# Two-layer diffusion backbone on one core: each engine's instruction order set by an event-by-event timing simulation instead of the scheduler's default model

## The chip, the cores and the metric

The kernel runs on one core of one Trainium2 chip. The metric is the device time of one execution in microseconds (us); the number that counts is the median of several runs. Beside the timed runs there is one execution taken by the hardware profiler, whose page and trace are read below. PE is TensorE (matrix multiplies), PEld its weight loads, DVE is VectorE, ACT is ScalarE, POOL is GpSimd, and SP is the engine that issues nearly all transfers.

## The reference

Two post-norm layers over 1024 latent tokens and 256 context tokens of width 1024, all in float32. Layer 0 (stage A below) is windowed grouped-query attention with a sink and rotary positions, layer 1 (stage B) is neighbourhood attention on a 16 x 64 grid with a relative bias. Both have a gate path. Cut to what matters:

```
for i in range(DEPTH):                       # DEPTH = 2
    shift, scale, gate = split(silu(c) @ w_ada[i] + b_ada[i], 3)
    u  = h * (1 + scale) + shift             # the same for the context tokens uc
    q, k, v, g = split(u @ w_in)
    s  = q @ k.T / 8  (+ mask or bias, + columns of the context, + sink)
    o  = softmax(s) @ v
    y  = (o * silu(g)) @ w_out
    h  = layer_norm(ALPHA * h + gate * y)
```

## The kernel before

**Precision.** Every float32 operand of a large product is split into a high part `hi` and a remainder `lo`, and the product is made of three matmuls: hi*hi, hi*lo and lo*hi. So each split costs an ACT cast (the high part) and a DVE or POOL subtraction (the low part).

**Stages.** From 0 to about 120 us the modulation vectors, the modulated tokens `uA` and the keys and values of layer 0 are made (lines 440 to 610). Stage A, about 120 to 620 us, is the attention of layer 0: 8 head pairs p, 10 blocks b of 128 queries, 2 heads each, which gives 160 softmaxes, numbered k in the names (`S_A84` is the score tile of softmax 84). From about 590 to 750 us come the output projection of layer 0, its layer norm and the tokens `uB` of layer 1. Stage B, about 830 to 1375 us, is the attention of layer 1 with 128 softmaxes; the rest is the last output projection and layer norm.

**One softmax.** `qkA`/`qkB` (L685, L686, L1016, L1017) makes the scores `S` on PE in four matmuls. `sm_first` lets DVE add mask or bias and find the row maximum (L315), and ACT take the exponential and its sum (L322). `sm_second` lets DVE invert the sum (L326) and POOL scale the row (L327). `sm_transpose` lets PE transpose the row into the tile `T`, up to five times 128 x 128 (L334), then ACT casts it into the high part `pth`/`pt` (L338) and DVE subtracts for the low part `ptl`/`pt` (L340). At last `pv` multiplies the high and the low part by the values (L714 in A, L1044, L1047 and L1050 in B) for two softmaxes at once, a pair k and k+1. Score tiles and transposed tiles take turns in the same two PSUM buffers (tag `big`, `bufs=2`): a new `S` or `T` needs the buffer of an older one, which is free when DVE has read the scores (L315) or has read the transposed tile (L340).

**Fill.** In between, the projections of the next heads are made (`proj_pieces`, L207 to L209, tiles `pj`; `vproj_pieces`, L240 to L242, tiles `pv` with a weight number), three matmuls per piece. These are called fill below: they need no softmax. In stage A, DVE also makes 112 dot products for the modulation of layer 1 (L600, L601) and the rotation of the new queries.

**What sets the order.** `build` states the instructions in a program order in which `merge` and `att_steps` weave attention and fill together by costs written into the code. That is not yet the order on the engines. When the tile context closes, its scheduler plays the program forward in simulated time: when an engine is free, it takes the instruction of the highest priority among those that can go, and gives its output tile a buffer. Priority is the place in program order; `tc.high_priority(n)`, called `lift` here, raises it for some steps (`LIFT_A` 80, `LIFT_B` 40, 20 and 60 in `sm_transpose`). So the durations and waits of the scheduler's timing model decide which of two instructions stands first on an engine, and each engine runs its list in that fixed order. The only line that the change touches is in `kernel`, where the context is made:

## Time and profile before

| what | value |
|---|---|
| median of 3 runs | 1474.33 us (1472.61 to 1474.68) |
| the profiled execution's own time | 1476.44 us |
| its span, first to last instruction | 1474.7 us |
| busy: PE / DVE / ACT / POOL | 95% / 71% / 49% / 42% |
| mean granted TensorE clock | 0.983 |
| instructions | 24806, of them 8660 matmuls |

The span is 1.7 us shorter than the profiled execution's time, which is itself 2.1 us above the median. A matmul's recorded duration is longer than the step from its start to the next one's start, since matmuls are pipelined; the start times tell the pace.

### The profile page before, as it was taken

The page shows a single profiled execution, that of the slowest core. Times are in us where ns is not written, and L with a number is a line of the kernel's source. Part 1 is how long each engine was busy: PE and PEld are TensorE (multiplying, and loading weights), DVE is VectorE, ACT ScalarE, POOL GpSimd, SP SyncE. Part 2 cuts the span into 40 slices and gives each one's busy share as a digit, 9 for nine tenths or more (in the row PEclk, how much of TensorE's full clock was granted, in tenths as well). Part 3 has the DMA queues.
Part 4 walks back from the last instruction along what each step waited for, and adds up shares of the span by engine and source line. Part 5 has one row for each costly group of instructions (what it writes and reads, how often), then busy time and mean ns, then how long its engine had stood idle before and what let it go on. Part 6 is the DMA issues. An engine that isn't in the chain of part 4 may idle for free.

```text
span 1474.7 us, 24806 instructions
## 1 busy us (share of the span) xinstructions
PE 1401.7 (95%) x8660; PEld 1231.5 (84%) x8660; DVE 1048.1 (71%) x2339; ACT 715.9 (49%) x1481; POOL 620.1 (42%) x739
## 2 busy tenths in 40 slices
PE   7898999999999999999999999999999999998995
PEld 5797888888888788878888889888998899877784
DVE  6957999988998988666632565655565555677788
ACT  4525566666666668633222444554454444457300
POOL 3433655555655546423311232332233323345564
PEclk6999999999999999999999999999999999999998
DMA  8455222311412213333267355555555465564443
GB/s 308 160 191 149 65 90 80 122 62 54 134 45 75 90 49 119 115 128 131 91 191 209 95 162 153 151 171 140 163 159 162 131 177 150 143 191 123 140 118 91
DMA packets 117084, 194.51 MB, mean 132 GB/s; under 512 B 9312, under 2 KB 57824, under 8 KB 116960
## 3 DMA queue, kind: packets, MB, share of 16 engines
q1 hardware_dynamic: 116960, 192.92, 43.7%
q8 instruction: 69, 1.13, 0.3%
q14 instruction: 55, 0.45, 0.1%
HBM read 140.98 MB, written 51.90 MB: 131 GB/s over the span
## 4 chain that ended last, share of the span: by engine, by line
PE 62%; DVE 19%; issue 6%; ACT 5%; DMA 4%; POOL 3%; SPq 0%; DVEq 0%; ACTq 0%; POOLq 0%
PE pj L207 8%; PE pj L209 8%; PE pj L208 8%; PE T_B L334 4%; PE pvB L1047 4%; DVE s_A L315 3%; PE T_A L334 3%; DVE ptl_A L340 3%; PE pv L240 3%; PE pv L241 3%; PE pv L242 3%; PE S_B L1016 3%; PE yA L419 2%; PE yA L417 2%; PE yA L418 2%
## 5 line engine op out<-in xcount | busy, mean ns | idle before, releaser
L327 POOL TENSOR_SCALAR s_B<-s_B,rs_B 128x640 f32<-128x640 f32 (+1 forms) x128 | 101.6, 794 | 304.0 <-DVE rs_B L326 281.2
L207 PE MATMUL pj<-uBh,wh 128*128 128x512 f32 (+1 forms) x448 | 176.2, 393 | 0.0
L322 ACT ACTIVATE s_A<-s_A,m_A 128x641 f32<-128x641 f32 (+2 forms) x160 | 119.6, 747 | 116.7 <-DVE m_A L315 94.8
L208 PE MATMUL pj<-uBl,wh 128*128 128x512 f32 (+1 forms) x448 | 169.5, 378 | 0.0
L209 PE MATMUL pj<-uBh,wl 128*128 128x512 f32 (+1 forms) x448 | 169.4, 378 | 0.0
L327 POOL TENSOR_SCALAR s_A<-s_A,rs_A 128x640 f32<-128x640 f32 (+2 forms) x160 | 137.5, 860 | 73.3 <-DVE rs_A L326 69.6
L340 DVE TENSOR_TENSOR pt_B<-T_B,pt_B 128x640 fp32r<-128x640 f32 (+1 forms) x128 | 101.0, 789 | 84.1 <-ACT pt_B L338 83.7
L322 ACT ACTIVATE s_B<-s_B,m_B 128x640 f32<-128x640 f32 (+1 forms) x128 | 102.9, 804 | 116.2 <-DVE m_B L315 114.8
L207 PE MATMUL pj<-uAh,wh 128*128 128x512 f32 (+1 forms) x384 | 141.6, 369 | 0.0
L315 DVE CUSTOM_DVE_ANT_0 s_A<-S_A,msk,nsk 128x640 f32<-128x640 f32 (+2 forms) x160 | 123.6, 773 | 22.4 <-PE S_A L686 13.7
L209 PE MATMUL pj<-uAh,wl 128*128 128x512 f32 (+1 forms) x384 | 138.3, 360 | 0.0
L208 PE MATMUL pj<-uAl,wh 128*128 128x512 f32 (+1 forms) x384 | 137.7, 359 | 0.0
L165 POOL TENSOR_TENSOR wl<-wr,wh 128x512 fp32r<-128x512 f32 x64 | 88.6, 1386 | 100.4 <-ACT wh L163 94.2
L340 DVE TENSOR_TENSOR ptl_A<-T_A,pth_A 128x640 fp32r<-128x640 f32 (+2 forms) x160 | 113.8, 711 | 6.3 <-ACT pth_A L338 3.8
L338 ACT CAST pt_B<-T_B 128x640 fp32r<-128x640 f32 (+1 forms) x128 | 84.4, 659 | 67.3 <-PE T_B L334 66.7
L334 PE MATMUL T_A<-ident,s_A 128*128 128x128 f32 x672 | 101.3, 275 | 14.0 <-DVE m_A L315 7.4
L334 PEld LDWEIGHTS T_A<-ident,s_A 128*128 128x128 f32 x672 | 78.0, 141 | 40.3 <-issue 15.2
L315 DVE CUSTOM_DVE_ANT_0 s_B<-S_B,bias 128x640 f32<-128x640 f32 (+1 forms) x128 | 100.5, 785 | 10.4 <-PE S_B L1017 9.6
L338 ACT CAST pth_A<-T_A 128x640 fp32r<-128x640 f32 (+2 forms) x160 | 96.7, 604 | 19.4 <-PE T_A L334 16.4
L209 PEld LDWEIGHTS pj<-uBh,wl 128*128 128x128 f32 x448 | 84.2, 188 | 16.7
L334 PE MATMUL T_B<-ident,s_B 128*128 128x128 f32 x608 | 88.1, 274 | 9.9 <-DVE pt_B L340 6.2
L240 PE MATMUL pv<-wh,uBh 128*128 128x256 f32 x320 | 92.1, 288 | 0.9 <-ACT wh L163 0.9
(189 smaller groups left out, 3916.5 us busy)
## 6 DMA issues: line engine op xcount, KB each, us to landing
kB<-kdB SPq DMA_DIRECT2D x64, 320.0 KB, 5.5
gw<-in_wadaT SPq DMA_DIRECT2D x64, 256.0 KB, 2.8
vdB<-st SPq DMA_DIRECT2D x20, 512.0 KB, 3.3
vB<-vdB SPq DMA_DIRECT2D x16, 640.0 KB, 4.6
kdB<-st SPq DMA_DIRECT2D x16, 512.0 KB, 2.9
qdB<-st SPq DMA_DIRECT2D x16, 512.0 KB, 3.3
qB<-qdB SPq DMA_DIRECT2D x32, 256.0 KB, 4.7
ogr<-ogd SPq DMA_DIRECT2D x28, 256.0 KB, 3.0
```

The source lines that it names most:

```text
L165: e.tensor_tensor(lo, r, f32(hi), ALU.subtract)
L207: mm(pt[:, :n], hi[:, sl], rh, start=kt == 0, stop=False)
L208: mm(pt[:, :n], hi[:, sl], rl, start=False, stop=False)
L209: mm(pt[:, :n], lo[:, sl], rh, start=False, stop=kt == KT - 1)
L240: mm(pt, lh, hi[:, sl], start=kt == 0, stop=False)
L315: nc.vector.tensor_tensor_reduce(outp, sc, in1, scale, init if init is not None else 3e38, ALU.add, ALU.min, accum_out=s.m)
L322: nc.scalar.activation(s.t[:, :n], s.t[:, :n], AF.Exp, bias=s.m, scale=-1.0, accum_out=s.sum)
L327: nc.gpsimd.tensor_scalar(s.t[:, : s.w], s.t[:, : s.w], s.rs, 1.0, ALU.mult, ALU.mult)
L334: nc.tensor.transpose(tp[:, k * P : (k + 1) * P], s.t[:, src * P : (src + 1) * P], ident)
L338: nc.scalar.copy(pt.hi[:, :n, hl, :], tv)
L340: nc.vector.tensor_tensor(pt.lo[:, :n, hl, :], tv, f32(pt.hi[:, :n, hl, :]), ALU.subtract)
L1047: mm(ov[:, :, 1], v[:, t, :], x[:, k], start=not side and k + n == 0, stop=k == 3 and n == 1)
```

## The change

The scheduler's timing model is exchanged when the context is made. Nothing else in the program differs: the same instructions on the same engines, the same buffers and the same lifts.

```
-    with tile.TileContext(nc) as tc:
+    with tile.TileContext(nc, schedule_with_timeline_sim=True) as tc:
```

The changed order was read next to the old one. These are three places of it.

First PE in stage A, at the end of a pair (`T_A84`, `T_A85`). `pth_A82` and `pth_A84` are the high parts of the pairs 82/83 and 84/85, `ptl_A82` is the low part of the older pair, `pj` is fill. Before:

```order
L334 MATMUL T_A85_4604<-ident_63,s_A85_4504 128x128 x5
L207 MATMUL pj26_2_4598<-uAh2_109,wh26_3869 128x256
L208 MATMUL pj26_2_4598<-uAl2_112,wh26_3869 128x256
L209 MATMUL pj26_2_4598<-uAh2_109,wl26_3870 128x256
L685 MATMUL S_A88_4615<-kA2_0_3726,qA8_4040 128x384
L686 MATMUL S_A88_4615<-kA2_0_3726,qA8_4040 128x256
L685 MATMUL S_A88_4615<-kA2_1_4294,qA8_4040 128x384
L686 MATMUL S_A88_4615<-kA2_1_4294,qA8_4040 128x256
L207 MATMUL pj26_2_4598<-uAh2_109,wh26_3869 128x256
L208 MATMUL pj26_2_4598<-uAl2_112,wh26_3869 128x256
L209 MATMUL pj26_2_4598<-uAh2_109,wl26_3870 128x256
L714 MATMUL pvA4_0_4551<-pth_A82_4486,vA2_3770 128x256 x5
```

Here the pair that PE multiplies after `T_A85` is the older one, 82/83; the pair 84/85 follows only after `T_A87`. Now, the same place:

```order
L334 MATMUL T_A84_4568<-ident_63,s_A84_4467 128x128 x5
L685 MATMUL S_A87_4576<-kA2_0_3726,qA9_4041 128x384
L686 MATMUL S_A87_4576<-kA2_0_3726,qA9_4041 128x256
L685 MATMUL S_A87_4576<-kA2_1_4294,qA9_4041 128x384
L686 MATMUL S_A87_4576<-kA2_1_4294,qA9_4041 128x256
L714 MATMUL pvA4_0_4551<-ptl_A82_4487,vA2_3770 128x256 x5
L334 MATMUL T_A85_4604<-ident_63,s_A85_4504 128x128 x5
L685 MATMUL S_A88_4615<-kA2_0_3726,qA8_4040 128x384
L686 MATMUL S_A88_4615<-kA2_0_3726,qA8_4040 128x256
L685 MATMUL S_A88_4615<-kA2_1_4294,qA8_4040 128x384
L686 MATMUL S_A88_4615<-kA2_1_4294,qA8_4040 128x256
L714 MATMUL pvA4_2_4734<-pth_A84_4566,vA2_3770 128x256 x5
```

The fill has left the attention steps and stands in long runs before and after them, and the product of a pair follows its second transpose with only one score tile in between.

Second DVE in stage A, between the score tiles 85 and 86 (`s_A` is the row of a softmax, `m_A` its maximum, `gw`, `gj` and `dhalf` belong to the dot products of the next layer's modulation). Before:

```order
L315 ISA s_A85_4504,m_A85_4505<-S_A85_4499,msk_145,nsk_146 128x640
L315 ISA m_A85_4505 128x1
L340 TENSOR_TENSOR ptl_A82_4487<-T_A82_4488,pth_A82_4486 128x5x128
L724 TENSOR_TENSOR otmp_4516<-pvA3_8_4406,otmp_4516 64x256
L326 RECIPROCAL rs_A85_4507<-sum_A85_4506 128x1
L601 ISA gw_4559,dhalf_615<-gw_4559,gh_3895 128x512
L601 ISA dhalf_615 128x1
L315 ISA s_A86_4541,m_A86_4542<-S_A86_4536,msk_145,nsk_146 128x640
```

One dot product stands between the two score tiles, and the softmax steps follow each other closely. Now:

```order
L315 ISA m_A85_4505 128x1
L276 SCALAR_TENSOR_TENSOR gA4_4443<-th_4690,pj26_2_4598 128x256
L600 ISA gj_4745,dhalf_615<-gw_4743,gh_3900 128x512
L600 ISA dhalf_615 128x1
L326 RECIPROCAL rs_A85_4507<-sum_A85_4506 128x1
L601 ISA gw_4743,dhalf_615<-gw_4743,gh_3895 128x512
L601 ISA dhalf_615 128x1
L600 ISA gj_4818,dhalf_615<-gw_4816,gh_3900 128x512
L600 ISA dhalf_615 128x1
L601 ISA gw_4816,dhalf_615<-gw_4816,gh_3895 128x512
L601 ISA dhalf_615 128x1
L315 ISA s_A86_4541,m_A86_4542<-S_A86_4536,msk_145,nsk_146 128x640
```

Four dot products stand there now, while PE is in a run of fill.

Third SP at the start, the first transfers after the weights `wr0` and `wr1` (`wada` and `hraw` feed the modulation and the tokens; `cos`, `sin`, `nsk` and `msk` are tables that the attention needs). Before:

```order
L517 DMA wada_254<-in_wadaS 128x1024
L522 DMA hraw_256<-in_hT 128x1280
L149 DMA wr2_258<-in_wAk 128x512
L149 DMA wr3_260<-in_wAk 128x512
L517 DMA wada_304<-in_wadaS 128x1024
L517 DMA wada_306<-in_wadaS 128x1024
L522 DMA hraw_308<-in_hT 128x1280
```

The four tables come some twenty transfers later, behind the last `hraw`. Now:

```order
L517 DMA wada_254<-in_wadaS 128x1024
L522 DMA hraw_256<-in_hT 128x1280
L522 DMA hraw_308<-in_hT 128x1280
L574 DMA cos_143<-in_cos 128x1024
L575 DMA sin_144<-in_sin 128x1024
L576 DMA nsk_146<-in_sink 128x16
L578 DMA msk_145<-in_maskA 128x1152
L517 DMA wada_304<-in_wadaS 128x1024
L149 DMA wr2_258<-in_wAk 128x512
L149 DMA wr3_260<-in_wAk 128x512
L517 DMA wada_306<-in_wadaS 128x1024
```

The tables have moved ahead of the third pair of modulation weights and of the weights `wr2` and `wr3`.

Counted over the whole lists: between the second transpose of a pair and the first product of that pair there stood ten or more fill matmuls for 71 of the 80 pairs of stage A, and no pair was without fill there; now 71 pairs have none (15 of them context blocks with tiles of 256 columns). Between one transpose and the next there was never less than one fill piece in A; now 83 of the 159 steps have none. In stage B the pairs without fill before their product go from 7 to 28 of 64, and the softmaxes that are transposed after the last projection matmul go from 19 to 23.

## The prediction

> **What bounds the kernel now.** The page comes first: its span, the busy times and the granted clock in 40 slices.

> ```profile
> span 1474.7 us, 24806 instructions
> PE 1401.7 (95%) x8660; PEld 1231.5 (84%) x8660; DVE 1048.1 (71%) x2339; ACT 715.9 (49%) x1481; POOL 620.1 (42%) x739
> PEclk6999999999999999999999999999999999999998
> ```

> PE is busy for 95% and has 73.0 us of idle time in all (1474.7 - 1401.7). No matmul is added or removed, so a new order can win no more than these 73 us, and it loses what it adds to them. Where they lie, the windows tell (length, busy time of PE, PEld, DVE, ACT and POOL with counts, granted clock, DMA share, GB/s).

> ```profile
> 0.00:50.00 50.00, 34.79 (x155) 27.69 (x156) 37.51 (x51) 20.82 (x38) 22.74 (x12) 0.71 0.75 273
> 120.00:616.00 496.00, 473.90 (x3044) 413.42 (x3045) 437.03 (x1092) 315.99 (x678) 281.08 (x408) 1.00 0.28 86
> 1000.00:1100.00 100.00, 100.00 (x706) 93.25 (x705) 57.68 (x140) 48.89 (x103) 32.46 (x38) 1.00 0.53 150
> 1300.00:1400.00 100.00, 90.34 (x540) 76.72 (x539) 75.05 (x154) 56.70 (x117) 55.08 (x52) 1.00 0.50 146
> 1400.00:1475.00 75.00, 57.60 (x275) 47.97 (x273) 63.70 (x79) 4.44 (x8) 41.13 (x19) 0.91 0.40 105
> ```

> The start loses 15.2 us. Stage A loses 22.1 of 496 us, and DVE is nearly as full there (437.0 of 496, 88%). The middle of stage B loses nothing. Its end, where fill has run out, loses 9.7 us in 100, and the last projection 17.4. Stage A is thus where both engines are close to full, and where the order has changed most. The view of waits names what PE's weight loads wait for there (total, times, longest).

> ```profile
> PEld T_A L334 <- issue: 15.2, 31, 2.8
> PEld S_A L685 <- DVE ptl_A L340: 11.3, 22, 1.5
> PEld T_A L334 <- POOL s_A L327: 10.4, 16, 2.5
> ```

> The score tile `S_A` waits for DVE to empty a PSUM buffer, the transpose for its row. These are small sums over 160 softmaxes, because fill stands between dependent steps. The timeline shows it (start, duration, engine, line; in brackets the idle time before and its releaser).

> ```profile
> 343.31 0.82 DVE L340 TENSOR_TENSOR ptl_A<-T_A,pth_A 128x640 fp32r<-128x640 f32 x1
> 344.18 0.45 PE L685 MATMUL S_A<-kA,qA 128*128 128x384 f32 x1 [0.52 <-DVE ptl_A L340]
> ...
> 346.85 0.71 PE L334 MATMUL T_A<-ident,s_A 128*128 128x128 f32 x5
> 347.31 0.42 PE L685 MATMUL S_A<-kA,qA 128*128 128x384 f32 x1
> 347.57 0.28 PE L686 MATMUL S_A<-kA,qA 128*128 128x256 f32 x1
> 347.64 0.69 ACT L338 CAST pth_A<-T_A 128x640 fp32r<-128x640 f32 x1 [0.53 <-PE T_A L334]
> 347.68 0.34 PE L685 MATMUL S_A<-kA,qA 128*128 128x384 f32 x1
> 347.86 0.28 PE L686 MATMUL S_A<-kA,qA 128*128 128x256 f32 x1
> 347.98 0.39 PE L207 MATMUL pj<-uAh,wh 128*128 128x512 f32 x1
> 348.21 0.39 PE L208 MATMUL pj<-uAl,wh 128*128 128x512 f32 x1
> 348.44 0.40 PE L209 MATMUL pj<-uAh,wl 128*128 128x512 f32 x1
> 348.68 0.76 PE L714 MATMUL pvA<-ptl_A,vA 128*128 128x256 f32 x5
> 349.27 0.39 PE L207 MATMUL pj<-uAh,wh 128*128 128x512 f32 x1
> ```

> After the transposes at 346.85, ACT's cast runs from 347.64 to 348.33; meanwhile PE makes one score tile (347.31 to 347.98) and goes on with fill at no loss. The row at 344.18 shows what happens where nothing stands between: PE pauses .52 us until DVE's subtraction has freed the buffer.

> **The change part by part.** The sum is made against the profiled 1476.4 us; 2.1 us come off at the end for the median.

> *Products of a pair behind its second transpose, stage A.* 71 pairs now have no fill there, only one score tile, as the order around `T_A85` shows; 15 of them are context blocks with short tiles, 56 have four or five transposes. By the rows above, the first product would stand at 347.98, and its high part is ready at 348.33: .35 us of pause. 56 x .35 = 20 us. The context blocks, whose tiles are 256 columns wide, I put at nothing, for their steps are half as long:

> ```profile
> L340 DVE TENSOR_TENSOR ptl_A<-T_A,pth_A 128x640 fp32r<-128x640 f32 x96 | 78.5, 818 | 3.0 <-ACT pth_A L338 1.9 <-PE pvA L714 0.5 <-issue 0.2
> ...
> L340 DVE TENSOR_TENSOR ptl_A<-T_A,pth_A 128x256 fp32r<-128x256 f32 x32 | 13.5, 422 | 3.1 <-ACT pth_A L338 1.6 <-issue 0.7 <-PE pvA L714 0.2
> ```

> *Transpose after transpose, stage A.* 83 steps have no fill now, 68 without the context blocks. A transposed tile needs the buffer of the previous one: cast end 348.33, plus .82 for the subtraction, so 349.15 at the earliest. PE has one score tile and five products in between (347.98 plus .59, from 348.68 to 349.27), which ends at 348.57, or at 348.92 where the pause of .35 has been taken already. It is short by .2 to .6 us; I take .3, nearer to the lower end, since most of these steps have the pause before them. 68 x .3 = 20 us.

> These two make 40 us. Against them stand the 22.1 us that A loses already: part of those are the same waits, now moved. I count 15 of them as replaced, roughly the `S_A` wait of 11.3 and part of the others, and take +25. The bounds lie far apart. Below: all 22 go and no new wait shows, -20. Above: each step costs what it costs at the end of B, where softmaxes run without fill.

> ```profile
> 1333.00:1353.00 20.00, 17.32 (x119) 14.92 (x120) 18.08 (x43) 16.35 (x36) 12.15 (x14) 1.00 0.50 152
> ```
> ```profile
> 1335.62 0.73 PE L334 MATMUL T_B<-ident,s_B 128*128 128x128 f32 x5 [0.31 <-DVE m_B L315]
> 1338.09 0.74 PE L334 MATMUL T_B<-ident,s_B 128*128 128x128 f32 x5 [0.35 <-DVE pt_B L340]
> ```

> One softmax takes 2.47 us there (1338.09 - 1335.62), while its matmuls start within .46 (transposes), .67 (scores) and .59 (products) by the rows of A, 1.72 in all: .75 us lost per step. 83 x .75 = 62, with the 20 for the products +82. I stay low because in A a run of only two to five softmaxes stands between long fill, so the chain starts ahead each time.

> *What DVE gains.* The dot products now run beside fill, away from the softmax steps, and partly away from POOL's scaling. Their groups come first, then the stretch ahead of the wait at 344.18, with one dot product beside POOL and two that ran by themselves:

> ```profile
> L601 DVE CUSTOM_DVE_ANT_0 gw<-gw,gh 128x512 f32<-128x512 f32 x64 | 50.9, 797 | 2.4 <-DMA gw<-in_wadaT 2.2
> L600 DVE CUSTOM_DVE_ANT_0 gj<-gw,gh 128x512 f32<-128x512 f32 x48 | 35.8, 745 | 0.5
> ```
> ```profile
> 340.38 0.69 ACT L338 CAST pth_A<-T_A 128x640 fp32r<-128x640 f32 x1
> ...
> 340.67 0.74 POOL L727 TENSOR_TENSOR gA<-otmp,gA 128x256 f32<-128x256 f32 x1
> 340.70 1.25 DVE L601 CUSTOM_DVE_ANT_0 gw<-gw,gh 128x512 f32<-128x512 f32 x1
> ...
> 342.69 0.68 DVE L600 CUSTOM_DVE_ANT_0 gj<-gw,gh 128x512 f32<-128x512 f32 x1
> ...
> 344.11 0.67 DVE L601 CUSTOM_DVE_ANT_0 gw<-gw,gh 128x512 f32<-128x512 f32 x1
> ```

> Alone they take .67 against means of .80 and .75: at most 64 x .13 + 48 x .08 = 12 us of DVE's 437. It shortens no PE work; I count it at nothing in the sum and as the ground of the faster rival. [...]

> *Stage B.* 21 more pairs without fill (7 to 28) at the same .35: +7. PE has no idle time there that they could replace, so 0 to +16 (at .75).

> *Tail.* The first softmax behind the last projection was `T_B109`, now `T_B105`: four more without cover. PE is busy 17.32 of 20 us there, 13% idle, .33 us of 2.47: +1.3, with the earlier lack of fill before `T_B121` and `T_B122` +2. Bounds 0 and +3 (4 x .75).

> *Start.* `cos`, `sin` and `msk` (512, 512 and 288 KB, 1.31 MB) now go ahead of modulation weights and of `wr2`, `wr3`. At the 273 GB/s of the first 50 us that is 4.8 us of transfer in front of what PE waits for. The tokens' second half comes earlier in return. 0 to +4.8; I take +3.

> Sum: +3 +25 +7 +2 = +37, so 1513.4 for a profiled execution and **1511** for the median.

> **The rivals.**

> *Absorbed.* In A, DVE is 88% busy and may itself be the clock of the stage; then waits only change their name and A costs nothing. For it: the 22.1 us idle already end mostly on DVE and POOL. Against: fill that kept PE busy is now used up elsewhere, and DVE has 59 us free. It gives 1474.3 + 12 = 1486.

> *Worse.* The long fill runs leave DVE without softmax work, and the attention runs pay the full chain. Then nothing of the 22.1 is replaced and the steps cost between .3 and .75: the median would lie between 1474.3 + 40 + 12 = 1526 and 1474.3 + 82 + 12 = 1568, middle 1547. It decides from about .5 us a step on. The tail's .75 speaks for it; that the chain is drained anew in each fill run speaks against.

> *Faster.* One mechanism: with the dot products put beside fill, DVE's queue is empty whenever a transposed tile is cast, each subtraction and maximum starts at once, and the buffer waits in A vanish. It would give back some 20 of the 22.1 us in A and 5 of the 9.7 at B's end, against +3 at the start: 1474.3 - 22 = 1452. For it: the .52 us wait at 344.18 is of the dot products' making, since the cast was done at 341.07 (340.38 + .69) and the subtraction came only at 343.31, behind the dot products of 340.70 and 342.69. Against it: even with an empty queue a buffer is taken from the transpose at 346.85 to 349.15, 2.30 us, and PE has 1.72 us of work for one softmax. It decides if cast and subtraction together fall from 1.5 to about .9 us, or if the order lets PE do a second score tile in that time.

> *Clock.* Pauses could make the throttle take the clock down, as at the start.

> ```profile
> 25.12 0.63 PE L559 MATMUL kp<-uAh,wh 128*128 128x512 f32 x1
> 25.55 0.63 PE L560 MATMUL kp<-uAh,wl 128*128 128x512 f32 x1
> ```

> A 512-column matmul took .43 us from start to start there, .23 in stage A (347.98 to 348.21). The first window's clock of .71 means 29 of 50 us at half speed; two such drops would add 29 us, 1540. The longest wait in A is 2.8 us and the clock there is 1.00, so pauses of that size did no harm. [...]

> *Not done.* If the order had stayed, nothing would move; the lists show it moved, so this is left with the case that all effects cancel.

> **How the numbers follow.** Forecast (1511, its own range 1495 to 1530) .47; absorbed .18; worse .14; faster .15; clock .03; no change .03. The range takes the bounds in: 1470 leaves out most of the faster case, 1560 the top of the worse one, together under .2. About 3 us (0.2%) can be told from no change by a measurement. Faster by more: .15. Within: .06, the .03 of no change and .03 of an absorbed case in which B, tail and start cost nothing either. Slower: .79.

> **What would show it right or wrong.** Right: PE's busy time stays near 1402 us, and its idle time between 120 and 620 us grows from 22 to about 47, as many pauses of .2 to .6 us ahead of `pvA` (released by ACT's cast) and of `T_A` (released by DVE's subtraction); stage B's middle is no longer at 100.00; the start is some 3 us later. Wrong: A's idle time at or under 22 us with DVE waiting for the cast (faster), or `S_A` waits replaced one for one (absorbed), or pauses over .7 us (worse). If the span moves while PE's idle time doesn't, the clock or the length of the matmuls has changed and my account fails.

## The result, and the profile after

The changed kernel takes 1624.66 us (median of 4 runs, 1624.08 to 1628.51) against 1473.8 us of the kernel before (1472.61 to 1474.68): a ratio of 1.1026 (95% interval 1.1009 to 1.1043). It is 151 us slower, four times the 37 us that were forecast, and past the end of the range (1560). The page of the profile after:

```profile
span 1622.3 us, 24857 instructions
PE 1459.9 (90%) x8660; PEld 1263.2 (78%) x8660; DVE 1045.0 (64%) x2339; ACT 717.7 (44%) x1481; POOL 600.0 (37%) x739
PEclk7899999899999999899999999999999999999997
```

Every count behind an x is the same as before; the 51 instructions more are waits for events. PE makes the same 8660 matmuls, yet is busy for 58 us longer, and its idle time has grown from 73 to 162 us. The windows, with the columns as in the prediction, chosen for the same stages:

```profile
0.00:50.00 50.00, 34.99 (x162) 27.52 (x162) 39.15 (x52) 21.02 (x38) 21.33 (x12) 0.76 0.89 325
120.00:726.00 606.00, 514.78 (x3039) 434.93 (x3037) 445.00 (x1094) 317.04 (x680) 273.00 (x409) 0.96 0.23 69
1100.00:1200.00 100.00, 98.66 (x682) 90.88 (x683) 54.36 (x138) 46.37 (x97) 29.66 (x36) 1.00 0.55 149
1400.00:1500.00 100.00, 81.33 (x481) 70.12 (x481) 65.84 (x149) 56.87 (x116) 40.12 (x46) 0.95 0.49 143
1522.00:1622.00 100.00, 83.91 (x391) 69.69 (x391) 84.01 (x102) 8.54 (x17) 55.06 (x28) 0.92 0.41 114
```

Stage A now needs 606 us for work that took 496; DVE's busy time there is almost unchanged (445.0 against 437.0). The granted clock of A is .96, no longer 1.00. Cut at four starts in the timeline (first score matmul of A, last transpose of A, first and last transposes of B), the span divides like this:

| us | before | after | difference |
|---|---|---|---|
| until the first score tile | 116.5 | 116.5 | 0 |
| stage A | 499.5 | 609.3 | +109.8 |
| between A and B | 210.9 | 209.7 | -1.2 |
| stage B | 548.8 | 586.9 | +38.1 |
| after the last transpose | 99.0 | 100.0 | +1.0 |
| of A at half speed (records of the clock) | 3.4 | 44.4 | +41.0 |

The view of waits tells what PE waits for (total, times, longest):

```profile
PE T_A L334 <- DVE m_A L315: 31.9, 34, 3.3
PE pvA L714 <- ACT pth_A L338: 24.8, 48, 1.4
...
PE pvB L1047 <- ACT pt_B L338: 12.6, 15, 3.3
...
PE T_A L334 <- DVE ptl_A L340: 8.8, 12, 2.4
...
PE S_A L685 <- DVE m_A L315: 7.7, 13, 1.4
```

The products wait for the cast as forecast (24.8 us; 20 were forecast). The transposes wait too, but above all for DVE's maximum of a score tile (`m_A`, 31.9 us, 7.4 before), and far less for the subtraction that the prediction had priced (`ptl_A`, 8.8 us). The timeline of one such wait:

```profile
404.09 1.28 POOL L165 TENSOR_TENSOR wl<-wr,wh 128x512 fp32r<-128x512 f32 x1 [1.68 <-ACT wh L163]
404.21 1.72 DVE L601 CUSTOM_DVE_ANT_0 gw<-gw,gh 128x512 f32<-128x512 f32 x1
404.75 0.71 PE L334 MATMUL T_A<-ident,s_A 128*128 128x128 f32 x5
405.21 0.42 PE L685 MATMUL S_A<-kA,qA 128*128 128x384 f32 x1
...
405.76 0.28 PE L686 MATMUL S_A<-kA,qA 128*128 128x256 f32 x1
405.86 1.22 DVE L600 CUSTOM_DVE_ANT_0 gj<-gw,gh 128x512 f32<-128x512 f32 x1
405.88 0.75 PE L714 MATMUL pvA<-ptl_A,vA 128*128 128x256 f32 x5
...
406.51 1.23 POOL L327 TENSOR_SCALAR s_A<-s_A,rs_A 128x640 f32<-128x640 f32 x1
...
407.56 0.71 DVE L601 CUSTOM_DVE_ANT_0 gw<-gw,gh 128x512 f32<-128x512 f32 x1
408.21 0.87 DVE L315 CUSTOM_DVE_ANT_0 s_A<-S_A,msk,nsk 128x640 f32<-128x640 f32 x1
...
409.01 0.81 DVE L340 TENSOR_TENSOR ptl_A<-T_A,pth_A 128x640 fp32r<-128x640 f32 x1
409.24 0.74 PE L334 MATMUL T_A<-ident,s_A 128*128 128x128 f32 x5 [2.60 <-DVE m_A L315]
...
411.89 1.27 PE L334 MATMUL T_A<-ident,s_A 128*128 128x128 f32 x5
```

The score tile was written by 406.04 (405.76 + .28). One dot product had just ended; DVE works through two more first and takes its maximum at 408.21. The subtraction that empties the older transposed tile runs only from 409.01 to 409.82, past the start of the transpose at 409.24. So the buffer that the transpose took is the score tile's, not the older transposed tile's. Its row came late as well, at 407.74, when POOL's scaling of 406.51 ended: 1.1 of the 2.60 us would have stayed without the buffer. PE has no fill to make meanwhile. Its next five transposes, 2.65 us later, last 1.27 instead of .74 us, since the clock has been halved. The windows of 2 us (granted clock third from the right) show it:

```profile
408.00:410.00 2.00, 0.76 (x6) 0.65 (x7) 1.97 (x6) 0.79 (x2) 1.55 (x2) 1.00 0.63 219
410.00:412.00 2.00, 1.72 (x10) 1.51 (x11) 1.68 (x5) 1.18 (x4) 0.98 (x2) 0.80 0.61 181
412.00:414.00 2.00, 2.00 (x11) 2.00 (x10) 0.42 (x2) 1.15 (x3) 0.71 (x2) 0.50 0.00 1
```

And the other half of the picture, a long fill run and the attention steps behind it:

```profile
430.00:435.00 5.00, 5.00 (x24) 4.14 (x23) 1.20 (x4) 0.18 (x1) 1.78 (x2) 1.00 1.04 228
435.00:444.00 9.00, 6.62 (x41) 5.09 (x40) 7.76 (x22) 6.16 (x15) 2.86 (x8) 1.00 0.48 126
```

In the fill run PE is full and DVE idle for 3.8 of 5 us; in the attention steps DVE is busy for 86% and ACT for 68%, and PE loses 2.4 of 9 us. Before, both kinds of work ran at once: 6 fill runs of over 2 us in A, 17 us together; now 48, 184 us.

### The profile page after: what moved, and what is told of

It reads as the page before. It is cut to its first block, busy times and chain, and to the rows that moved or that the text cites. A ratio compares the mean times of both kernels' runs of the same rounds, so it can differ in the third digit from the quotient of the medians.

```text
span 1622.3 us, 24857 instructions
## 1 busy us (share of the span) xinstructions
PE 1459.9 (90%) x8660; PEld 1263.2 (78%) x8660; DVE 1045.0 (64%) x2339; ACT 717.7 (44%) x1481; POOL 600.0 (37%) x739
## 4 chain that ended last, share of the span: by engine, by line
PE 59%; DVE 16%; DMA 10%; ACT 7%; issue 6%; POOL 1%; SPq 1%; DVEq 0%; ACTq 0%; POOLq 0%
PE pj L207 9%; PE pj L208 8%; PE pj L209 8%; PE pvB L1047 3%; PE T_B L334 3%; PE pvA L714 3%; DVE s_A L315 3%; PE yA L417 2%; PE yA L419 2%; PE yA L418 2%; PE T_A L334 2%; PE S_B L1016 2%; DVE ptl_A L340 2%; PE pv L240 2%; PE pv L241 2%
## 5 line engine op out<-in xcount | busy, mean ns | idle before, releaser
L327 POOL TENSOR_SCALAR s_B<-s_B,rs_B 128x640 f32<-128x640 f32 (+1 forms) x128 | 101.2, 790 | 248.4 <-DVE rs_B L326 220.8
L207 PE MATMUL pj<-uBh,wh 128*128 128x512 f32 (+1 forms) x448 | 172.2, 384 | 2.8 <-ACT wh L163 2.8
L208 PE MATMUL pj<-uBl,wh 128*128 128x512 f32 (+1 forms) x448 | 170.5, 381 | 0.0
L209 PE MATMUL pj<-uBh,wl 128*128 128x512 f32 (+1 forms) x448 | 170.1, 380 | 0.0
L315 DVE CUSTOM_DVE_ANT_0 s_A<-S_A,msk,nsk 128x640 f32<-128x640 f32 (+2 forms) x160 | 123.4, 771 | 70.9 <-PE S_A L686 65.1
L315 DVE CUSTOM_DVE_ANT_0 s_B<-S_B,bias 128x640 f32<-128x640 f32 (+1 forms) x128 | 100.6, 786 | 100.6 <-PE S_B L1017 98.5
L327 POOL TENSOR_SCALAR s_A<-s_A,rs_A 128x640 f32<-128x640 f32 (+2 forms) x160 | 129.6, 811 | 87.0 <-DVE rs_A L326 84.0
L338 ACT CAST pth_A<-T_A 128x640 fp32r<-128x640 f32 (+2 forms) x160 | 96.7, 605 | 128.6 <-PE T_A L334 126.7
L334 PE MATMUL T_A<-ident,s_A 128*128 128x128 f32 x672 | 106.2, 284 | 51.6 <-DVE m_A L315 31.9
L340 DVE TENSOR_TENSOR pt_B<-T_B,pt_B 128x640 fp32r<-128x640 f32 (+1 forms) x128 | 100.5, 786 | 69.1 <-ACT pt_B L338 68.8
L207 PE MATMUL pj<-uAh,wh 128*128 128x512 f32 (+1 forms) x384 | 138.9, 362 | 0.0
L340 DVE TENSOR_TENSOR ptl_A<-T_A,pth_A 128x640 fp32r<-128x640 f32 (+2 forms) x160 | 113.7, 711 | 37.6 <-ACT pth_A L338 37.1
L209 PE MATMUL pj<-uAh,wl 128*128 128x512 f32 (+1 forms) x384 | 137.6, 358 | 0.0
L208 PE MATMUL pj<-uAl,wh 128*128 128x512 f32 (+1 forms) x384 | 137.3, 358 | 0.0
L334 PEld LDWEIGHTS T_A<-ident,s_A 128*128 128x128 f32 x672 | 78.0, 145 | 73.5 <-issue 26.3
L338 ACT CAST pt_B<-T_B 128x640 fp32r<-128x640 f32 (+1 forms) x128 | 85.0, 665 | 110.0 <-PE T_B L334 109.1
L165 POOL TENSOR_TENSOR wl<-wr,wh 128x512 fp32r<-128x512 f32 x64 | 83.6, 1308 | 114.1 <-ACT wh L163 98.7
L320 POOL COPY s_A<-nsk 128x1 f32<-128x1 f32 x160 | 46.3, 290 | 185.5 <-PE T_A L334 185.1
L334 PE MATMUL T_B<-ident,s_B 128*128 128x128 f32 x608 | 89.4, 277 | 19.0 <-DVE m_B L315 15.1
L685 PE MATMUL S_A<-kA,qA 128*128 128x384 f32 (+1 forms) x256 | 92.1, 380 | 9.7 <-DVE m_A L315 7.7
```

The lines of the kernel that those rows point to most:

```text
L165: e.tensor_tensor(lo, r, f32(hi), ALU.subtract)
L207: mm(pt[:, :n], hi[:, sl], rh, start=kt == 0, stop=False)
L208: mm(pt[:, :n], hi[:, sl], rl, start=False, stop=False)
L209: mm(pt[:, :n], lo[:, sl], rh, start=False, stop=kt == KT - 1)
L315: nc.vector.tensor_tensor_reduce(outp, sc, in1, scale, init if init is not None else 3e38, ALU.add, ALU.min, accum_out=s.m)
L327: nc.gpsimd.tensor_scalar(s.t[:, : s.w], s.t[:, : s.w], s.rs, 1.0, ALU.mult, ALU.mult)
```

## The experiments

Main theory: fill no longer stands between the dependent steps, and each step left bare pays its chain. Rivals: the raised priorities (lifts) are lost, the order on DVE is at fault, the clock. Ratios are against the kernel before, timed beside each run. "Default" runs have the old timing model, "event" runs the changed line. "Bare steps" go from one transpose to the next without fill, "bare pairs" have no fill between the second transpose and the first product; both are counted in the order lists of A. Stage A's length and half-speed time come from the trace, cut as above.

| run | median us | ratio (interval) | A us | B us | half speed in A us | bare steps, pairs |
|---|---|---|---|---|---|---|
| before | 1473.8 | 1 | 499.5 | 548.8 | 3.4 | 0, 0 |
| changed | 1624.7 | 1.1026 (1.1009 to 1.1043) | 609.3 | 586.9 | 44.4 | 83, 71 |
| 1 default, no lifts | 1491.2 | 1.0107 (1.0091 to 1.0123) | 512.6 | 554.9 | 17.1 | 0, 0 |
| 2 event, every piece held | 1522.5 | 1.0320 (1.0301 to 1.0339) | 533.4 | 562.5 | 30.7 | 7, 7 |
| 3 event, every second held | 1570.1 | 1.0632 (1.0594 to 1.0669) | 580.1 | 566.1 | 64.9 | 52, 32 |
| 4 event, no dots | 1611.5 | 1.0921 (1.0903 to 1.0939) | 596.2 | 587.7 | 44.4 | 81, 70 |
| 5 default, no dots | 1467.3 | .9952 (.9935 to .9969) | 490.1 | 549.7 | 10.2 | 0, 0 |
| 6 default, program order | 1510.5 | 1.0242 (1.0224 to 1.0261) | 524.3 | 555.5 | 10.2 | 0, 1 |
| 7 default, clumps of 6 | 1573.4 | 1.0678 (1.0656 to 1.0700) | 583.8 | 557.1 | 23.9 | 81, 13 |
| 8 event, buffer free earlier | 1603.7 | 1.0871 (1.0847 to 1.0894) | 587.9 | 587.0 | 61.4 | 78, 64 |
| 9 default, every piece held | 1492.3 | 1.0120 (1.0099 to 1.0141) | 509.7 | 555.3 | 10.2 | 4, 4 |
| 10 default, clumps of 4 | 1555.4 | 1.0541 (1.0518 to 1.0563) | 575.5 | 554.8 | 44.4 | 54, 1 |
| 11 event, added matmuls | 1635.2 | 1.1093 (1.1068 to 1.1117) | 620.2 | 588.2 | 27.3 | 77, 69 |
| 12 event, fill and dots held | 1518.7 | 1.0298 (1.0282 to 1.0313) | 526.2 | 561.7 | 27.3 | 7, 7 |

**Run 1, the default model without lifts.**

```
-        return tc.high_priority(n) if n else nullcontext()
+        return nullcontext()
```

> The kernel before with its default model, but every raise of priority (lift) taken out. It asks whether the event-by-event order is slow because it pays no heed to the raised priorities (the order of the changed kernel does not change by one instruction when the lifts are taken out). Rival theory, lost lifts: then the default model without them must lose about as much, 1600 to 1630 us. Main theory, missing fill: what counts is whether fill stands between the dependent steps; here no pair of stage A is without fill and no step from transpose to transpose (before: none and none; changed: 71 and 83), so 1470 to 1490 us.

Measured 1491.2 us, 15 over the kernel before (1475.75 beside it): 13 more in stage A, 6 in B, a little less elsewhere. The lists of the changed kernel are the same on PE, DVE, ACT and POOL with the lifts taken out as with them, so in the event-by-event order they do nothing; but under the default model their loss is worth about a tenth of the 151 us. The rival falls as the main cause and stays as a term of up to some 15 us.

**Run 2, event by event, every fill piece held.** The first matmul of a piece is held behind the matmul that the program states ahead of it (the same in `vproj_pieces`).

```
-    with tile.TileContext(nc) as tc:
+    with tile.TileContext(nc, schedule_with_timeline_sim=True) as tc:
...
-                    mm(pt[:, :n], hi[:, sl], rh, start=kt == 0, stop=False)
+                    tc.keep_in_program_order(mm(pt[:, :n], hi[:, sl], rh, start=kt == 0, stop=False))
```

> The changed kernel, with the first matmul of every fill piece held behind what the program states ahead of it on PE, so that fill can no longer be drawn ahead of attention steps; all other engines and all attention steps are still ordered event by event. Pairs of stage A without fill before their product: 7 (changed kernel 71), steps from transpose to transpose without fill 7 (83). Main theory, missing fill: the 150 us nearly vanish, 1470 to 1500 us, idle time of PE in stage A back under 35 us, and no half-speed stretches in stage A. Rival, DVE's order (dot products in clumps among the softmax steps): that order is still event by event, so at least half of the loss stays, over 1550 us. Rival, lost lifts: the lifts still have no effect, over 1550 us.

Measured 1522.5 us: 102 of the 151 us are gone, 76 in A and 24 in B, by holding fill alone. The stage A window:

```profile
120.00:650.00 530.00, 484.82 (x3044) 426.56 (x3042) 436.66 (x1090) 315.75 (x677) 267.43 (x408) 0.97 0.25 78
```

PE's idle time in A is 45 us (91 in the changed kernel), not under 35, and 30.7 us at half speed remain. So the main theory holds for two thirds, and the expectation was too low by 20 us and more. Both rivals asked for over 1550 us here and fall as main causes.

**Run 3, every second piece held.**

```
-                    tc.keep_in_program_order(mm(pt[:, :n], hi[:, sl], rh, start=kt == 0, stop=False))
+                    x = mm(pt[:, :n], hi[:, sl], rh, start=kt == 0, stop=False)
+                    if kq % 2 == 0:
+                        tc.keep_in_program_order(x)
```

> As the run with every piece held, but with only every second fill piece held, so that fill stands in longer runs. Stage A: 32 pairs without fill before their product, 52 steps from transpose to transpose without fill (of 71 and 83 in the changed kernel, 7 and 7 with every piece held). Stage B is nearly as with every piece held. Main theory, missing fill, about 1.3 us a bare step: stage A 45 more bare steps than with every piece held, some 45 to 60 us over that run, 1520 to 1560 us. If the loss were of the other engines' order, this run would lie as high as the changed kernel; if it is a matter of a few bad places, as low as the run with every piece held.

Measured 1570.1 us, 47.6 over run 2, nearly all of it in A (+46.7). The loss goes with the number of bare steps, at about 1.04 us for a step with its share of pairs and of the clock: half-speed time in A rose by 34 us, worth at most 17 (in the changed kernel a step of 512 columns took .427 us at half speed and .228 at full). The total is 10 us above the range expected, since run 2 lay higher than supposed.

**Runs 4 and 5, no dot products,** event by event and by default. Both `tensor_tensor_reduce` calls of `dot_half` are left out, and the sums set to zero.

```
-                nc.vector.tensor_tensor_reduce(o, t, gh[1], 0.5, 0.0, ALU.mult, ALU.add, accum_out=acc[:, j, 1:2])
+                pass
...
-            nc.vector.tensor_tensor_reduce(t, t, gh[0], 0.5, 0.0, ALU.mult, ALU.add, accum_out=acc[:, j, 0:1])
```

> The changed kernel without the 112 dot products of DVE in stage A (they are left out, and zeros stand for their sums, so the modulation of layer 1 is not computed; their transfers stay). PE's order stays nearly the same (72 pairs and 84 steps without fill). Main theory, missing fill: the chain from transpose to free buffer gets a little shorter, since DVE has less in its queue, but the bare steps stay bare: 1585 to 1615 us. Rival, DVE's order: the dot products that now stand in clumps among the softmax steps hold up the subtractions and maxima; without them most of the loss goes, 1480 to 1550 us.

> Control to the changed kernel without dot products (1611.5 us, 13 under the changed kernel): the kernel before without the 112 dot products of DVE in stage A (left out, zeros stand for their sums; their transfers stay). Main theory: fill covers nearly all of DVE's queue, so little to win, 1466 to 1474 us. Rival, DVE's order costs the changed kernel more than the kernel before: then this control wins clearly less than the 13 us. If it wins as much, the dot products are no cause of the loss at all.

Counted as for the other runs, the first has 81 bare steps and 70 bare pairs. Measured 1611.5 us (13 less than the changed kernel) and 1467.3 us (ratio .9952, some 7 us less). By these two times the new place of the dot products costs about 6 us more than the old one. But the edit brings a stall of its own. Nothing reads the `gw` tiles any more, their transfers are issued in long rows, and ACT's tanh for the second half of the dot products (L594) waits for one of them; behind it stand DVE, POOL and PE. In run 4:

```profile
169.88 0.63 ACT L594 ACTIVATE gth<-gh 128x512 f32<-128x512 f32 x1 [17.55 <-DMA gw<-in_wadaT]
172.46 1.30 PE L334 MATMUL T_A<-ident,s_A 128*128 128x128 f32 x5 [16.82 <-POOL s_A L327]
```

In run 5 the same place holds PE for 3.8 us. So the dot products are worth 13 to some 30 us in the changed kernel and 7 to some 11 before, and their new place 6 to some 19. They are no main cause either way. The rest of DVE's order is not tested by this run; runs 7 and 10 bear on it.

**Runs 6, 7 and 10, the changed kernel's PE order rebuilt under the default model.** Every group of matmuls of stage A is held to the order of the program (shown for one), and `merge` states fill in clumps of 1, 6 and 4 pieces.

```
+            if k == 0 and name[0] == "A":
+                tc.keep_in_program_order(x)
...
-                cf += fill[jf][0]
-                fill[jf][1]()
-                jf += 1
+                for _ in range(clump if jf + clump <= len(fill) else 1):
+                    cf += fill[jf][0]
+                    fill[jf][1]()
+                    jf += 1
```

> Control to the next run. The kernel before with its default model, but PE in stage A held to the order of the program: the first matmul of every fill piece, score tile, transpose group and product is held behind what is stated ahead of it. Stage A: 1 pair without fill before its product, no bare step from transpose to transpose. Main theory, missing fill: near the kernel before, 1475 to 1505 us (the lifts no longer act on PE).

> As the run before it (default model, PE held to the order of the program in stage A), but the program states fill of stage A in clumps of six pieces. This rebuilds the changed kernel's PE order under the default model: 81 bare steps from transpose to transpose (changed kernel 83) and 13 pairs without fill before their product (71). DVE, ACT and POOL are still ordered by the default model with its lifts. Main theory, missing fill, at 1.0 to 1.3 us a bare step: 70 to 110 us over the control, 1550 to 1610 us, with half-speed stretches in stage A. Rival, the other engines' event-by-event order is the cause: within 25 us of the control.

> Default model, PE in the order of the program in stage A, fill stated in clumps of four: 54 bare steps from transpose to transpose, but only 1 pair without fill before its product. It prices the bare step alone. From the three differences measured so far (clumps of six against program order, +59.5 us in stage A for 81 steps and 12 pairs; changed kernel against every piece held, +75.9 for 76 and 64; every second against every piece, +46.7 for 45 and 25) a step comes to .68 us and a pair to .38: 54 x .68 = 37 over the control, so 1540 to 1556 us, stage A near 561 us. If the price hangs on something else than the count (the length of the runs, the clock), it falls outside.

Measured 1510.5, 1573.4 and 1555.4 us. The control is 5 us above its range: PE in program order without lifts costs 36 us by itself. Against it clumps of six cost 62.9 us (59.5 in A, 81 bare steps and 12 more pairs: .73 us a step if the pairs cost nothing), clumps of four 44.9 us (51.2 in A, 54 bare steps and no more pairs: .95 a step). The profiled execution with clumps of four was 4.5 us above its median; by the medians a step costs .78 and .83 us. Clumps of four are inside their range in total, but stage A came to 575.5 us where 561 was expected, so the step was priced too low there as well. The waits of transposes for the maximum, of the control and of the clumps of six (line numbers are one higher in these kernels):

```profile
PE T_A L335 <- DVE m_A L316: 14.0, 27, 1.4
```
```profile
PE T_A L335 <- DVE m_A L316: 53.4, 59, 1.9
```

DVE, ACT and POOL are ordered by the default model here, and yet the loss and its kind come back with the bare steps: stage A is 84 us longer than in the kernel before, 25 of them already in the control, against 110 in the changed kernel. That PE's order makes most of the loss in A is thereby shown; the event-by-event order of the other engines is not needed for it. Clumps of four cost more per step than clumps of six, and also ran 44.4 us at half speed against 23.9.

**Run 8, the buffer free after the cast.**

```
-            nc.vector.tensor_tensor(pt.lo[:, :n, hl, :], tv, f32(pt.hi[:, :n, hl, :]), ALU.subtract)
+            nc.vector.tensor_tensor(pt.lo[:, :n, hl, :], f32(pt.hi[:, :n, hl, :]) if a else tv, f32(pt.hi[:, :n, hl, :]), ALU.subtract)
```

> The changed kernel, but in stage A DVE makes the low part from the high part alone (so it is zero and half of the precision is left out; the operation keeps its size): the transposed tile's PSUM buffer is then free after ACT's cast and no longer after DVE's subtraction. 78 bare steps from transpose to transpose (83), 64 pairs without fill (71). Two-buffer theory: the bare steps are long because a transposed tile holds one of the two PSUM buffers for 3.0 us on average, 1.5 us of that for DVE's subtraction; freed earlier, stage A loses 40 to 70 us less, 1555 to 1585 us. Rival, PE waits for softmax rows and for the cast before the product, not for buffers: less than 20 us gained, over 1605 us.

Measured 1603.7 us, 21 less; between the two theories' ranges. Two things blur it: A ran 17 us longer at half speed, which hides up to 8.5 us of the gain, and there are 5 bare steps fewer. PE's waits of this run:

```profile
PE T_A L334 <- ACT pth_A L338: 18.8, 24, 2.4
PE S_A L685 <- ACT pth_A L338: 18.1, 24, 1.6
PE S_A L685 <- DVE m_A L315: 12.5, 18, 3.8
```

PE still waits for buffers, now for ACT's cast to free them. Taking one step out of the chain lets the next one end last; the subtraction alone does not set the bare step.

**Run 9, every fill piece held under the default model**: run 2's edit without the event-by-event order.

> Control to the event-by-event run with every fill piece held (1522.5 us): the same holds under the default model, lifts in force. It asks what is left of the loss there (47 us over the kernel before) and whether the holding itself costs it. If the holding costs: 1505 to 1525 us. If what is left is of the event-by-event order (no lifts, 15 us by the run without them, and DVE, ACT and POOL in another order): 1474 to 1492 us. Stage A has 4 pairs and 4 steps without fill.

Measured 1492.3 us, at the upper edge of the second range: under the default model the holding costs 18 us by itself. So of the 47 us that run 2 kept, about 18 may be of the holds and about 30 are of the event-by-event order of the rest.

**Run 11, work added in the pauses.** `BARE_A` lists the 83 softmaxes.

```
+        if extra is not None:
+            for _ in range(3):
+                mm(tp[:, 640:1024], extra[:, 0:128], extra[:, 0:384], start=True, stop=True)
...
+        extra = qA[2 * p + h] if k in BARE_A else None
```

> The changed kernel with work added: behind the transposes of each of the 83 bare steps of stage A, three more matmuls of 384 columns into the unused columns of the transposed tile (about .5 us each time, 43 us in all; results unused). PE then pauses less. Clock theory: in the changed kernel stage A runs 44 us at half the clock, after stretches in which PE was less than about half busy; the added work keeps PE busy, the half-speed stretches become fewer than half, and although 43 us of work are added the time stays within 10 us of the changed kernel or falls below it, 1595 to 1635 us. If the clock does not depend on it, the half-speed time stays near 44 us; if the pauses are not there to be used, the time rises by 30 to 43 us, 1650 to 1670 us.

Measured 1635.2 us, 10.5 over the changed kernel and at the upper end of the clock theory's range, for 249 more matmuls (249 x .175 = 44 us of work by the usual step of 384 columns). Its stage A:

```profile
120.00:738.00 618.00, 543.73 (x3290) 471.28 (x3289) 444.81 (x1097) 321.52 (x684) 272.60 (x409) 0.98 0.23 68
```

Half-speed time fell from 44.4 to 27.3 us, not to under half; three quarters of the added work went into pauses or was paid back by the clock. The added work also changed the order: 77 bare steps instead of 83, some 5 us by the prices above. The three can't be parted by this run. It agrees with the clock theory in sign; 17 us less at half speed are worth at most 8.5.

**Run 12, fill and dot products held.** The edit of run 2, and `tc.keep_in_program_order` around the two calls left out in run 4.

> The event-by-event run with every fill piece held (1522.5 us), with the dot products of DVE held too, each behind what the program states ahead of it on DVE, so that they no longer stand in clumps ahead of the maxima. If DVE's order is what is left of the loss there: 1490 to 1510 us, and PE's waits for the maximum of the scores in stage A (17 us there) fall under half. If it is the lost lifts and the late key loads: 1515 to 1525 us.

Measured 1518.7 us, 4 less than run 2, and PE's waits of transposes for the maximum went from 17.0 to 12.7 us, not to under half. The dot products are not what is left of the loss there.

## Why the prediction was wrong

**What it had right.** The stage, the direction and the mechanism in A: PE's bare steps, shown by holding fill (runs 2 and 3) and by taking it away under the default model (runs 7 and 10). The start was small as said (+3 forecast, 0 measured), and the sum was carried by stage A, as said. The tail's +2 lies within stage B as cut here and was not measured apart.

**Stage A term by term.** The starts of the matmuls part its time. The usual step from one start to the next is .108 us for 128 columns, .117 for 256, .175 for 384 and .228 for 512; at half speed it was .213 for 128 and for 256, .321 for 384 and .427 for 512 (medians of the changed kernel, 1.8 to 2 times as long), and the surplus has a row of its own. What goes beyond this by over .15 us is called a pause.

| us in stage A | before | after | difference | forecast |
|---|---|---|---|---|
| all matmuls at their usual step | 447.4 | 447.4 | 0 | |
| pauses ahead of transposes | 19.6 | 64.3 | +44.7 | +20 |
| pauses ahead of a pair's first product | 0 | 34.4 | +34.4 | +20 |
| pauses ahead of score tiles | 14.7 | 19.2 | +4.5 | -15 (old idle time of every kind) |
| doubled steps at half speed | 1.4 | 16.2 | +14.8 | 0 |
| the rest, delays below .15 us | 16.4 | 27.8 | +11.4 | |

**The step that failed** is "Transpose after transpose, stage A", the term 68 x .3 = 20 us, where 45 came. It took the buffer to be that of the previous transposed tile, and its chain from one instance with empty queues (346.85 to 349.15). The wait that ends last is mostly DVE's maximum of the score tile in the other buffer. With all that comes with it, a bare step costs .73 to .95 us (runs 7 and 10). Over the whole of A the trace of before already had a longer figure than 2.30 us: a transposed tile held its buffer for 3.4 us on average from its first transpose to the end of the subtraction, since cast and subtraction stand in queues; fill had hidden that. In the changed kernel it is 3.0 us, against 1.72 us of PE work for a softmax (means over the 160 tiles). By the upper bound of .75, which the prediction had from the end of B and put away, 83 x .75 + 20 = 82 us. Its reason to stay low, "the chain starts ahead each time", does not hold: from one transpose group to the next, less the usual steps between, the first bare step behind fill loses 1.33 us on average and the second 1.19.

**The product of a pair** was right in kind but not in size. Of the longer pairs, 46 pause by .58 us on average, where 56 by .35 were forecast; and of the context blocks, put at nothing, nine pause by .82.

**The old idle time** was set off at 15 us as replaced. No kind of pause shrank. Only their causes changed: the first matmul of a score tile waits less for the subtraction (5.3 to 1.8 us in the view of waits) and more for the maximum of an older tile (2.0 to 7.7). The new waits came on top.

**Stage B** was forecast at +7 and measured at +38. The pairs had been counted by the product of L1047. In B the products of L1044 stand ahead of it for 28 of the 64 pairs, and they need both parts. Counted by the first product, 48 of 64 pairs are bare, not 28, and from transpose to transpose 26 steps, not 12: 41 pairs at .35 and 14 steps at .75 would have given 25 us. B also ran at half speed for 13.7 us, none before, which is worth at most 7. Run 2 got back 24 of the 38.

**The clock** had .03 and nothing in the sum. Nine stretches in A, 44.4 us together, ran at half speed, and cost some 15 of the 110 us. The prediction argued from a longest wait of 2.8 us that did no harm. It misread its own trace: that wait ended at 130.31, and half speed followed at 130.38 for 3.41 us, which the mean of 1.00 over 496 us rounds away. In the kernel before:

```profile
126.97:130.38 3.41, 0.99 (x6) 0.50 (x5) 1.68 (x5) 1.97 (x5) 0.01 (x1) 1.00 0.60 151
130.38:133.79 3.41, 3.41 (x13) 3.12 (x14) 2.00 (x4) 1.55 (x3) 1.74 (x3) 0.50 0.95 265
```

In the changed kernel a pause of 2.60 us ended at 409.24, and the clock fell at 411.21. The 3.41 us ahead of each of the nine drops in A had PE busy for 19 to 52%.

**The dot products** were to free up to 12 us of DVE by leaving POOL's scaling. Their means rose instead, from 797 to 874 and from 745 to 792 ns, since they met POOL's other work: the one at 404.21 ran 1.72 us and ended .56 us after POOL's subtraction of 404.09. Of the 112 dot products, 28 took over 1 us, 15 before; each of these ended about .55 us after an operation of POOL, which for 18 of the 28, and for 9 of the 15 before, was not the scaling (L327). Those that met none took .69. What makes a dot product longer beside POOL was not shown.

**Not in the prediction at all**: the event-by-event order pays no heed to the lifts (up to 15 us, by run 1 under the default model).

**The test by PE's busy time** failed too: it was to stay near 1402 us and rose to 1459.9. A matmul's record lasts longer than its step to the next start (.45 us for 384 columns at 438.08 and the next start .29 later), so the head of each pause counts as busy, and half speed lengthens records (a median of .63 instead of .39 us for 512 columns). Idle time therefore understates what pauses cost; start-to-start times do not.

**The rivals.** "Worse" was the case that came, at 1547 with .14, and its top of 1568 was still 57 us short. Stage A lies 28 us over the 82 of that top, B with the tail 29 over the 9 forecast, and the start 3 under; the clock and the lost lifts are inside these. The last 3 us are of medians against profiled executions. "Absorbed" and "faster" fell.

**What stays open.** Of the 151 us, 102 are of fill drawn ahead (run 2 against the changed kernel). The 47 that run 2 keeps are lifts (up to 15), the holds' own cost (up to 18), dot products (4 by run 12), and a remainder; these terms overlap and were not parted further. Why the event-by-event simulation draws fill ahead was not tried. A third buffer for scores and transposes was not tried either.

## What to carry to other kernels

An order that packs independent work into long runs leaves the dependent steps bare: look in the order lists for steps between which nothing else stands, and price each by the mean time that its buffer is held under load too, not only by one instance with empty queues. Here the mean of before less PE's own work (3.4 - 1.72) bounds the step from above, and the one instance (.3) from below. Where two engines are each nearly full in a stage (PE 96%, DVE 88%), let them run at once; where they took turns here, the stage grew from 499.5 to 609.3 us. When a scheduler's model is exchanged, see first whether the priorities written into the code still move anything.

## What was not expected of the hardware

A DVE dot product that takes .69 us alone took up to 1.73 us beside POOL, and up to 1.78 before the change.
